# A hybrid encoder layer on one core: gate block maxima at heads five to eight, query and key rows of the second memory in other buffers, the first sequence's output begun behind its last row

## The chip, the core and the metric

The kernel runs on one core of a Trainium2 chip. The core has a matmul engine (TensorE, PE in the profile; PEld is its weight load), a vector engine (VectorE, DVE), an engine for activation functions and copies (ScalarE, ACT), a general-purpose engine (GpSimd, POOL) and an engine that here issues nearly all transfers (SyncE, SP). Each engine works through its own instructions in order and waits on semaphores for the others. The metric is the device time of one launch in microseconds (us); the three runs of the kernel before took 2096.93, 2098.42 and 2098.59 us, a median of 2098.42.

## What is computed

Two sequences of 512 tokens with 1024 channels go through the same encoder layer. In short:

```python
x = x + 0.5 * swiglu(rms_norm(x, ffn1_norm), ffn1_w_gate, ffn1_w_up, ffn1_w_down)
h = rms_norm(x, mix_norm)
aq, ak, av, mq, mk, mv, gate_pre, o_pre, g_att, g_mlstm = split(h @ w_in)
att = gqa_block_attention(rope(rms_norm(aq)), rope(rms_norm(ak)), av)      # 8 heads of 64, 2 key heads
mem = mlstm_bidirectional(mq, mk, mv, gate_pre, gate_bias, o_pre, head_norm)  # 4 heads of 128
merged = sigmoid(g_att) * (att @ w_up_att) + sigmoid(g_mlstm) * (mem @ w_up_mlstm)
x = x + merged @ w_out
x = x + 0.5 * swiglu(rms_norm(x, ffn2_norm), ffn2_w_gate, ffn2_w_up, ffn2_w_down)
y = rms_norm(x, final_norm)
```

Everything is float32. The memory (mlstm) has gates per token; for every memory head and each of its two directions the kernel needs the largest gate exponent in each block of 128 tokens, with and without a triangular mask. These are the block maxima of the title.

## The kernel before

**Precision.** A float32 operand is split into a high part and the rest (`split`, lines 656 to 658, and `split_w`, 236 to 241: ACT copies the high part, DVE subtracts), and a product is three matmuls: high by high, high by low, low by high. Weights of the mixing block are split once for the first sequence and parked in memory; the second sequence loads the two parts back (`load_w`, lines 247 to 263; in the profile `wpark<-w` at L262 and `w<-wpark` at L254).

**Stages.** The program starts with the first feed-forward block (FFN) of both sequences together, whose gate, up and down products go through a scheme that needs seven products where eight would do it directly. Then comes the mixing block (`mix`), as a generator for each sequence: `m0` for the first, `m1` for the second, which are advanced in turn, so that the second's projections run beside the first's output projection. Then comes the second FFN of both sequences together, and with its last products the final norm and the write-out.

**Order.** The instructions of one engine are not in the order of the text. A planner sorts them ahead of the launch: every instruction has a priority, which counts up along the text; `shifted(n)` adds n to it for a while (a positive number is later). An instruction that is ready may be taken ahead of one with an earlier priority that isn't. On the chip the planned order of each engine is fixed.

**Buffers.** On-chip memory is given out in rings by tag. Those that matter here: `wr`, four buffers for raw weights; `w8`, four buffers of twice that size for split weights; `t2` and `f2`, rows of 128 x 512; the banks `mm` (3), `s` (2, in the profile `pss`), `t` (2, `pst`) and `o` (1, `pso`) of the matmul's accumulators. `box` is one tile of eight rows, cut by hand into four rows for gate exponents (`eb`) and four for output gates.

**The mixing block**, as far as the change touches it. `gates` (line 860) computes the gate exponents and writes them to memory (`ebuf`). `mem_rows` (lines 956 to 964) loads one head's and direction's exponents into a row of `box` for all partitions (`box<-ebuf`, L959) and adds the mask (L963: on POOL for the first sequence, on DVE for the second). `mem_max` (lines 966 to 969) takes the block maxima of both rows with two DVE reductions into `n1` and `bd` (L968, L969; the tile is `st`). `mem_scales` (from line 971) makes the memory's scales out of all of them, and `mem_head` (from line 1102) uses these for a head: it loads the rows again, computes ACT exponentials (L1126), multiplies them with the product of the head's query and key rows (L1112, L1128), and `mem_out` turns the result and multiplies it with the values.

The query and key rows of memory head h come from two projections, `mem_qk(h, 0)` and `mem_qk(h, 1)` (line 909): each result is scaled (L914) and split into a high and a low row (L657, L658). The four rows lie in one tile of ring `w8`, `qks[h]`. For heads one and two they are projected before the attention, for heads three and four while the memory heads run.

The attention runs head by head: `scores(h + 1)` (matmuls L997 into the two `s` banks, row maximum on DVE L1000, exponential on ACT L1002, reciprocal and scaling on DVE L1003 and L1004), then `attend(h)` (turning L1016, split, product with the values L1024), then one `mem_max`, and then `fill`, which lets one or two further projections of the queue follow, one for the first four heads and two for the others.

**The start.** The first sequence's rows are turned on PE (`turn`, L1233), its norm factors are computed on DVE and ACT (`rows_rstd`), and `bcast_psum` (lines 209 to 214) brings the factors into all partitions with four transposes (L213); only then can DVE scale the rows (L1257).

**The end.** `ffn_down` (from line 505) runs 28 steps of four blocks of nine (or six) matmuls; every block ends in an addition on DVE (L606). The last rows of the first sequence come out of the last step but two (T4), the upper half of the second sequence's out of the last but one (T1), the rest out of the last (B22), which is cut in two halves of 256 columns. With each row of the first sequence `done2` adds its squares to a sum (`sq_add`, L155 on ACT and L156 on POOL). `finish0` computes the norm factor of the first sequence (`stats`: transposes L203, a reduction L205 and twelve small operations) and turns, scales (L1416) and writes its eight output tiles.

Of the kernel before, what the change touches and what calls it, by code (L numbers as in the profile page):

```python
# [9 lines left out]
F32R = mybir.dt.float32r  # L10
# [6 lines left out]
P = 128  # L17
S = 512
D = 1024
KD = D // P  # L20
# [6 lines left out]
def encoder(ctx, tc, I, outs):  # L27
    nc = tc.nc
# [3 lines left out]
    wpool = ctx.enter_context(tc.tile_pool(name="wpool", bufs=3))  # L32
# [9 lines left out]
    def nm(s):  # L42
        n_id[0] += 1
        return f"{s}_{n_id[0]}"

    @contextmanager
    def shifted(n):

        tc.cur_priority += n
        yield  # L50
        tc.cur_priority -= n
# [603 lines left out]
    def split(src, hi, lo, eng=None):  # L655

        nc.scalar.activation(hi, src, AF.Copy)  # L657
        (eng or V_).tensor_tensor(lo, src, f(hi), op=ALU.subtract)  # L658
# [101 lines left out]
    def mix(s, xh, xl, early=None, extra=None, after=None):  # L760
# [147 lines left out]

        def mem_qk(h, j):
            def done(pp):  # L910
                if j == 0:
                    qks[h] = wpool.tile([P, 4, S], F32R, tag="w8", bufs=4, name=nm("qk"))
                t = F2()
                V_.tensor_tensor(t, pp, R[s], op=ALU.mult)  # L914
                split(t, qks[h][:, 2 * j, :], qks[h][:, 2 * j + 1, :])
            return win_cols((768, 1280)[j] + h * P, done)

        ogs = {}
# [47 lines left out]
        def mem_max(h, d):  # L966
            eb3, em3 = mem_rows(h, d)
            V_.tensor_reduce(n1[:, d, :, h], em3, axis=AX.X, op=ALU.max)  # L968
            V_.tensor_reduce(bd[:, d, :, h], eb3, axis=AX.X, op=ALU.max)  # L969
# [78 lines left out]
        for h in range(HA):  # L1048
            nxt = scores(h + 1) if h + 1 < HA else None
            attend(h, Ps)  # L1050
            Ps = nxt
            with shifted(150):
                mem_max(h // 2, h % 2)
            fill(1 if h < 4 else 2)
            if h == 2 and extra:
                extra()
# [45 lines left out]
        def mem_head(h):  # L1102
            qk = qks[h]
            ebs, ems = zip(*[mem_rows(h, d) for d in range(2)])
            dn_ = small(8, "dn")
            dn = dn_.rearrange("p (d b) -> p d b", d=2)
            Ts = []
            for i in range(4):
                p = PS()
                isl = slice(i * P, (i + 1) * P)  # L1110
                for n, (a, b) in enumerate(((0, 2), (0, 3), (1, 2))):
                    nc.tensor.matmul(p, qk[:, a, isl], qk[:, b, :], start=(n == 0), stop=(n == 2))  # L1112
                pair = []
                for d in range(2):
                    W = T2()
                    st_ = i if d == 0 else 3 - i
                    for j in range(st_ + 1):
                        b = j if d == 0 else 3 - j
                        if j == st_:
                            src, bias = ems[d][:, j], bd[:, d, st_, h:h + 1]  # L1120
                        else:
                            src = ebs[d][:, j]
                            dist = st_ - j
                            bias = (n1[:, d, st_, h:h + 1] if dist == 1 else
                                    n2[:, d, st_, h:h + 1] if dist == 2 else n2[:, d, 1, h:h + 1])
                        nc.scalar.activation(W[:, b * P:(b + 1) * P], src, AF.Exp, bias=bias)  # L1126
                    cl = slice(0, (i + 1) * P) if d == 0 else slice(i * P, S)
                    V_.scalar_tensor_tensor(W[:, cl], p[:, cl], DM ** -0.5, W[:, cl], op0=ALU.mult, op1=ALU.mult,  # L1128
                                            accum_out=dn[:, d, st_:st_ + 1])
                    pair.append(W)  # L1130
                Ts.append(pair)
            V_.scalar_tensor_tensor(dn_, dn_, -1.0, dn_, op0=ALU.mult, op1=ALU.max)
            V_.tensor_tensor(dn, dn, en[:, :, :, h], op=ALU.max)
            V_.reciprocal(dn_, dn_)
            for i in range(4):
                tf, tb = Ts[i]
                rf, rb = dn[:, 0, i:i + 1], dn[:, 1, 3 - i:4 - i]
                lo_, di_, up_ = slice(0, (i + 1) * P), slice(i * P, (i + 1) * P), slice((i + 1) * P, S)
                nc.scalar.activation(tf[:, lo_], tf[:, lo_], AF.Copy, scale=rf)
                V_.scalar_tensor_tensor(tf[:, di_], tb[:, di_], rb, tf[:, di_], op0=ALU.mult, op1=ALU.add)  # L1140
                if i < 3:
                    V_.tensor_scalar(tf[:, up_], tb[:, up_], rb, None, op0=ALU.mult)
            return Ts
# [122 lines left out]
    for k, bank in enumerate((MM, PS, PT, MM, PS, PT, MM, PO)):  # L1266
        keep_x(0, k, turn(0, k, bank), x0r[k])
    W = [gu_left_a(raw0[0])]
    R0 = bcast_psum(rs)
    xc[B11], xc[B21] = xc_tile(), xc_tile()  # L1270

    def first_x(k):
# [188 lines left out]

    def done2(s, d, th):
        if s == 0:
            acc0[0] = sq_add(xs[0][:, d, :], acc0[0], "R")
        elif d == KD - 1:
            finish0()
            finish1_upper()
        elif th is not None:
            finish1(th)
# [44 lines left out]
```

## Time and profile before

| | |
|---|---|
| median of three runs | 2098.42 us |
| the profiled execution | 2097.18 us |
| its span, first to last instruction | 2095.4 us |
| its mean granted TensorE clock | 0.997 |
| PE busy | 2066.0 us (99%) |
| DVE busy | 1575.3 us (75%) |
| ACT busy | 895.9 us (43%) |
| POOL busy | 104.7 us (5%) |
| DMA moved | 458.53 MB, mean 219 GB/s |
| chain that ended last: PE | 90% |

A line of a timeline reads: start in us, duration in us, engine, line of the kernel, operation, what it writes <- what it reads, shapes, number of instructions put together; in brackets, the idle time of the engine before it and what ended that. On DVE and ACT the listed durations of instructions that follow each other overlap by some 0.1 us; from start to start a 128 x 512 operation on DVE takes 0.6 us. "SPq" is a transfer being issued by SP. A line of the waits reads: who <- for whom: us in total, times, longest. A line of a stretch of time reads: its bounds, its length, then busy time and number of instructions of PE, PEld, DVE, ACT and POOL, the granted clock of PE, the share of the DMA engines that was busy, and GB/s.

### The profile page before, as it was taken

The numbers are of one execution on the slowest core, as the hardware profiler recorded it, in microseconds if no ns is written. First come the engines' busy times: TensorE is split into PE (matmuls) and PEld (weight loads), VectorE is DVE, ScalarE is ACT, GpSimd is POOL, SyncE is SP. The second block draws the span as 40 slices with busy tenths as digits, with TensorE's granted clock in tenths as the row PEclk, the third lists the DMA queues.
The fourth block names the chain that finished last, engine by engine and source line by source line (L and its number), as shares of the span: only waits on it lengthen the run. The fifth ranks groups of instructions, "written<-read, shape, count | busy, mean of one in ns | idle before, by whom it ended". The sixth has DMA issues, their size and how long they took to land.

```text
span 2095.4 us, 27335 instructions
## 1 busy us (share of the span) xinstructions
PE 2066.0 (99%) x9488; PEld 1694.0 (81%) x9488; DVE 1575.3 (75%) x2866; ACT 895.9 (43%) x1645; POOL 104.7 (5%) x110
## 2 busy tenths in 40 slices
PE   8999999999999999999999999999999999999997
PEld 6888888888888777878887787888888888888886
DVE  7888988786797898575568745545888888786796
ACT  7544444442235566463334543323544444443222
POOL 0000000001003011000110000001000000000000
PEclk9999999999999999999999999999999999999999
DMA  9655655699767655769585354677656555599752
GB/s 282 200 179 183 204 170 181 208 348 352 259 229 253 212 180 176 260 229 302 176 298 165 101 172 157 204 247 248 207 171 212 190 173 181 190 348 348 259 192 110
DMA packets 304187, 458.53 MB, mean 219 GB/s; under 512 B 20305, under 2 KB 170849, under 8 KB 303025
## 3 DMA queue, kind: packets, MB, share of 16 engines
q1 hardware_dynamic: 303456, 455.52, 64.5%
q0 software_dynamic: 592, 1.27, 0.3%
q8 instruction: 75, 1.23, 0.3%
q14 instruction: 64, 0.52, 0.1%
HBM read 289.82 MB, written 166.89 MB: 218 GB/s over the span
## 4 chain that ended last, share of the span: by engine, by line
PE 90%; DVE 4%; DMA 3%; ACT 1%; issue 1%; SPq 0%; DVEq 0%; POOL 0%; ACTq 0%
PE mm L755 17%; PE pss L333 17%; PE pst L333 11%; PE mm L333 10%; PE mm L589 8%; PE pst L589 4%; PE pss L589 4%; PE mm L739 4%; PE pso L589 3%; PE pso L739 1%; PE pso L1024 1%; PE pst L1016 1%; PE pss L997 1%; PE pst L755 1%; PE pss L755 1%; PE pss L1112 1%
## 5 line engine op out<-in xcount | busy, mean ns | idle before, releaser
L755 PE MATMUL mm<-xh,w 128*128 128x512 f32 x896 | 293.2, 396 | 1.4 <-DMA w<-wpark 1.4
L333 PE MATMUL pss<-xc,w 128*128 128x512 f32 x1056 | 256.4, 392 | 0.3 <-DVE t L364 0.3
L333 PE MATMUL mm<-xc,w 128*128 128x512 f32 x1056 | 252.7, 390 | 1.6 <-ACT w L291 0.9
L333 PE MATMUL pst<-xc,w 128*128 128x512 f32 x1056 | 253.6, 389 | 0.0
L333 PEld LDWEIGHTS pss<-xc,w 128*128 128x128 f32 x1056 | 196.8, 188 | 47.7 <-DVE t L364 7.2
L333 PEld LDWEIGHTS mm<-xc,w 128*128 128x128 f32 x1056 | 197.4, 188 | 44.3 <-ACT w L291 1.8
L333 PEld LDWEIGHTS pst<-xc,w 128*128 128x128 f32 x1056 | 198.2, 188 | 41.2
L755 PEld LDWEIGHTS mm<-xh,w 128*128 128x128 f32 x896 | 168.1, 189 | 36.3 <-DMA w<-wpark 2.7
L589 PE MATMUL mm<-rt,w 128*128 128x512 f32 (+1 forms) x819 | 187.7, 383 | 0.0
L755 PE MATMUL mm<-xl,w 128*128 128x512 f32 x448 | 176.5, 394 | 0.0
L589 PEld LDWEIGHTS mm<-rt,w 128*128 128x128 f32 x819 | 150.6, 188 | 29.8
L291 ACT ACTIVATE w<-t 128x512 fp32r<-128x512 f32 x176 | 107.1, 627 | 140.5 <-issue 55.2
L292 DVE TENSOR_TENSOR w<-t,w 128x512 fp32r<-128x512 f32 x176 | 118.4, 688 | 50.3 <-ACT w L291 48.1
L333 PE MATMUL pss<-xc,f 128*128 128x512 f32 x528 | 126.8, 389 | 0.0
L333 PEld LDWEIGHTS pss<-xc,f 128*128 128x128 f32 x528 | 99.1, 188 | 20.6
L657 ACT ACTIVATE w<-wr 128x512 fp32r<-128x512 f32 x72 | 45.1, 632 | 138.3 <-PE pso L589 65.2
L755 PEld LDWEIGHTS mm<-xl,w 128*128 128x128 f32 x448 | 84.5, 189 | 16.7
L657 ACT ACTIVATE w<-t 128x512 fp32r<-128x512 f32 x82 | 51.8, 631 | 107.4 <-PE pst L589 62.4
L589 PE MATMUL pss<-rt,w 128*128 128x512 f32 x396 | 93.6, 389 | 0.0
L589 PE MATMUL pst<-rt,w 128*128 128x512 f32 x396 | 93.6, 389 | 0.0
L239 ACT ACTIVATE w<-wr 128x1024 fp32r<-128x1024 f32 (+1 forms) x56 | 57.3, 1028 | 74.5 <-PE mm L755 32.0
L589 PEld LDWEIGHTS pst<-rt,w 128*128 128x128 f32 x396 | 74.3, 188 | 15.4
(333 smaller groups left out, 3675.4 us busy)
## 6 DMA issues: line engine op xcount, KB each, us to landing
rt<-rbuf SPq DMA_DIRECT2D x154, 512.0 KB, 5.5
wpark<-w SPq DMA_DIRECT2D x104, 512.0 KB, 3.5
w<-wpark SPq DMA_DIRECT2D x104, 512.0 KB, 4.9
wr<-in_ffn_w_gate_dram SPq DMA_DIRECT2D x62, 512.0 KB, 5.5
rbuf<-tab SPq DMA_DIRECT2D x102, 256.0 KB, 4.3
wr<-in_ffn_w_up_dram SPq DMA_DIRECT2D x44, 512.0 KB, 4.6
rbuf<-f SPq DMA_DIRECT2D x72, 256.0 KB, 4.1
wr<-in_w_in_dram SPq DMA_DIRECT2D x36, 512.0 KB, 6.9
```

Of the source, the lines that this page charges most:

```text
L239: pin(nc.scalar.activation(hi, raw, AF.Copy))
L291: pin(nc.scalar.activation(t[:, 0], src, AF.Copy))
L292: pin(V_.tensor_tensor(t[:, 1], src, f(t[:, 0]), op=ALU.subtract))
L333: nc.tensor.matmul(p, a[:, k, :], xt[:, b, k, :], start=(first and k == 0 and i == 0), stop=(k == HK_ - 1 and i == 2), skip_group_check=True)
L589: nc.tensor.matmul(p, u[:, a, d * P:(d + 1) * P], r[:, b, ts], start=(first and q == 0 and k == 0), stop=(q == len(us) - 1 and k == 2), sk ...
L657: nc.scalar.activation(hi, src, AF.Copy)
L739: nc.tensor.matmul(p[b][:, :N], a[:, k, bs], w_[:, kl, :], start=(k == 0 and i == 0), stop=(k == KD - 1 and i == 2))
L755: nc.tensor.matmul(p, a[:, k, :], b, start=(k == 0 and i == 0), stop=(k == n - 1 and i == 2))
L997: nc.tensor.matmul(p, qT[:, h, b * P:(b + 1) * P], kv[:, hk * 2 + j, :], start=(j == 0), stop=(j == 1))
L1016: nc.tensor.transpose(p[:, b * P:(b + 1) * P], Ps[b][:, kb * P:(kb + 1) * P], ident)
L1024: nc.tensor.matmul(po, Vst[:, kv_, hk, :], w, start=(kv_ == 0 and i == 0), stop=(kv_ == 3 and i == 1))
L1112: nc.tensor.matmul(p, qk[:, a, isl], qk[:, b, :], start=(n == 0), stop=(n == 2))
```

## The change

Four things are changed.

1. `mem_max` is no longer called once after every attention head with a priority 150 later; it is called twice after each of heads five to eight, for both directions of memory head h - 4, with no shift.
2. In the second sequence (`s` is 1) the four rows of a memory head no longer lie in one tile of ring `w8`, but in two tiles of two rows, one for each projection, in ring `wr`. In the first sequence they stay where they were; the rows are only named one by one.
3. The broadcast of the first sequence's norm factors at the start of the program gets a priority 60 earlier.
4. `finish0` is called behind the first sequence's last row, in step T4, with a priority 100 later, and no longer behind the upper half of the second sequence's, in step T1. The sums of squares of its last four rows are added by DVE and no longer by POOL.

```diff
         def mem_qk(h, j):
             def done(pp):
-                if j == 0:
-                    qks[h] = wpool.tile([P, 4, S], F32R, tag="w8", bufs=4, name=nm("qk"))
+                if j == 0 and not s:
+                    t = wpool.tile([P, 4, S], F32R, tag="w8", bufs=4, name=nm("qk"))
+                    qks[h] = [t[:, i] for i in range(4)]
+                elif s:
+                    t = wpool.tile([P, 2, S], F32R, tag="wr", bufs=4, name=nm("qk"))
+                    qks.setdefault(h, []).extend(t[:, i] for i in range(2))
                 t = F2()
                 V_.tensor_tensor(t, pp, R[s], op=ALU.mult)
-                split(t, qks[h][:, 2 * j, :], qks[h][:, 2 * j + 1, :])
+                split(t, *qks[h][2 * j:2 * j + 2])
...
             attend(h, Ps)
             Ps = nxt
-            with shifted(150):
-                mem_max(h // 2, h % 2)
+            if h >= 4:
+                mem_max(h - 4, 0)
+                mem_max(h - 4, 1)
             fill(1 if h < 4 else 2)
...
                 for n, (a, b) in enumerate(((0, 2), (0, 3), (1, 2))):
-                    nc.tensor.matmul(p, qk[:, a, isl], qk[:, b, :], start=(n == 0), stop=(n == 2))
+                    nc.tensor.matmul(p, qk[a][:, isl], qk[b], start=(n == 0), stop=(n == 2))
...
-    R0 = bcast_psum(rs)
+    with shifted(-60):
+        R0 = bcast_psum(rs)
...
         if s == 0:
-            acc0[0] = sq_add(xs[0][:, d, :], acc0[0], "R")
+            acc0[0] = sq_add(xs[0][:, d, :], acc0[0], "R", eng=V_ if d >= DH else None)
+            if d == KD - 1:
+                with shifted(LATER):
+                    finish0()
         elif d == KD - 1:
-            finish0()
             finish1_upper()
```

## The prediction

> **What bounds the kernel now.** I read the page first, then the waits of the matmul engine over the whole span, and then the stretches of time in which those waits lie.
>
> ```profile
> span 2095.4 us, 27335 instructions
> PE 2066.0 (99%) x9488; PEld 1694.0 (81%) x9488; DVE 1575.3 (75%) x2866; ACT 895.9 (43%) x1645; POOL 104.7 (5%) x110
> ```
>
> PE (TensorE) is busy 99% of the span, and the change takes no matmul away. So it can only win what PE loses: 2095.4 - 2066.0 = 29.4 us of idle time, about 10 us of it the last write-out after the last matmul, and whatever PE does at a lowered clock. The waits (total, times, longest, in us) say where:
>
> ```profile
> PE pss L997 <- ACT t L1002: 3.4, 2, 3.1
> PE pst L937 <- DVE t L658: 1.9, 2, 1.2
> PE pss L1405 <- DVE xs L606: 1.4, 1, 1.4
> PE mm L755 <- DMA w<-wpark: 1.4, 3, 0.7
> ```
>
> L997 is the score matmul of an attention head, L937 the turning of the queries, L1405 the last write-out, L755 a projection that waits for parked weights. Four stretches of time (length, busy time of PE, PEld, DVE, ACT, POOL, then granted clock, DMA share, GB/s) show what stands behind them: heads one to four of the first and of the second sequence, heads five to eight of the second, and the stretch before the end.
>
> ```profile
> 706.00:760.00 54.00, 52.81 (x258) 41.56 (x257) 53.03 (x101) 31.98 (x68) 6.86 (x5) 1.00 0.61 195
> 1106.00:1160.00 54.00, 50.09 (x230) 39.46 (x230) 48.57 (x123) 26.98 (x62) 0.00 (x0) 0.94 0.51 155
> 1160.00:1216.00 56.00, 55.81 (x282) 43.96 (x281) 34.89 (x69) 27.50 (x59) 0.70 (x1) 1.00 0.35 117
> 2066.60:2086.20 19.60, 17.19 (x141) 16.02 (x139) 17.32 (x54) 5.85 (x21) 0.00 (x0) 1.00 0.33 122
> ```
>
> In heads one to four DVE is full (53.03 of 54, 48.57 of 54) and PE loses 1.2 and 3.9 us; in heads five to eight of the second sequence DVE has 21 us to spare and PE loses 0.2. Before the end DVE is again close to full and PE loses 2.4.
>
> **Part 1, the block maxima, second sequence.** This is the largest term. PE, at the first head's scores:
>
> ```profile
> 1106.05 1.07 PE L997 MATMUL pss<-kv,qT 128*128 128x512 f32 x4
> ...
> 1108.54 0.39 PE L755 MATMUL mm<-xl,w 128*128 128x512 f32 x1
> 1112.05 0.89 PE L997 MATMUL pss<-kv,qT 128*128 128x512 f32 x2 [3.12 <-ACT t L1002]
> ...
> 1115.42 0.45 PE L1016 MATMUL pst<-ident,t 128*128 128x128 f32 x1 [0.77 <-DVE asm L1003]
> ```
>
> ```profile
> 1112.00:1120.00 8.00, 7.18 (x21) 5.24 (x21) 4.76 (x13) 2.23 (x6) 0.00 (x0) 0.57 0.81 267
> ```
>
> Two gaps, 3.12 and 0.77 us, and then a granted clock of 0.57: 7.18 us of matmul time at 0.57 loses 7.18 x 0.43 = 3.1 us more. What DVE did meanwhile, and what SP issued:
>
> ```profile
> 1108.05 0.69 DVE L963 TENSOR_TENSOR box<-box,tab 128x512 f32<-128x512 f32 x1 [0.37 <-DMA box<-ebuf]
> 1108.66 0.68 DVE L969 TENSOR_REDUCE st<-box 128x4 f32<-128x512 f32 x1
> 1109.26 0.68 DVE L968 TENSOR_REDUCE st<-box 128x4 f32<-128x512 f32 x1
> 1109.85 0.68 DVE L914 TENSOR_TENSOR f<-mm,R 128x512 f32<-128x512 f32 x1
> 1110.45 0.68 DVE L1000 TENSOR_REDUCE asm<-pss 128x1 f32<-128x512 f32 x1
> ```
>
> ```profile
> 1104.27 3.74 SPq L232 DMA_DIRECT2D wr<-in_ffn_w_gate_dram  x1
> 1108.12 1.79 SPq L959 DMA_DIRECT2D box<-ebuf  x1
> ```
>
> L963, L968 and L969 are one block maximum (mem_max). L1000, the row maximum of the first scores, has its first bank from about 1106.6 on (two of the four matmuls at 1106.05) and runs at 1110.45 behind two of these maxima, one of which waits for its DMA; the DMA of the next sits behind a weight transfer that holds SP for 3.74 us. The scores that find no bank start at 1112.05, which is 1.6 us after L1000. Without the maxima L1000 follows L914 at about 1107.5, and the scores start near 1109.1, right behind the last L755: of the 3.12 us some 0.2 stay. So the gain is 2.9 + 0.77 + 3.1: **-6.8 us**. The bounds are -7.0, all of it, and 0 when the maxima stay where they are (first rival). Moved to heads five to eight they are the same 8 x 3 instructions of 0.6 us each, 14.4 us, against the 21 us that DVE has idle there, and PE has two filling projections a head to cover them.
>
> The Trainium skill, "TensorE: Matmul & The Clock Gate", sections "HAM oscillation — how this bites in real kernels" and "What's actually happening", says that an idle gap of some 3.4 us puts the matmul clock back to half, and that about 3.4 us of work restore it. The 0.57 behind a gap of 3.12 us agrees in kind. By its figure the lowered clock would cost 3.4 x 0.5 = 1.7 us (an estimate from that page) instead of 3.1, and the whole sum would come out 1.4 us smaller; this case's row lasts longer, and I go by the row.
>
> **Part 1, first sequence.** Here the adds (L963) run on POOL and only the two reductions on DVE.
>
> ```profile
> 704.55 0.63 PE L937 MATMUL pst<-ident,t 128*128 128x128 f32 x4 [1.16 <-DVE t L658]
> ```
>
> ```profile
> 701.70 0.68 DVE L969 TENSOR_REDUCE st<-box 128x4 f32<-128x512 f32 x1
> ...
> 714.36 0.67 DVE L968 TENSOR_REDUCE st<-box 128x4 f32<-128x512 f32 x1
> ```
>
> One reduction of 0.6 us stands on DVE in front of each of the two splits (L658) that PE waits for (1.9 us together). Taking both away: **-1.2 us**; bounds -1.9 and 0. The sixteen reductions do not get fewer; in heads five to eight they compete with the same attention work, for which the third rival has the price. The scales that follow the maxima (mem_scales) come later, and so do the first memory head's exponentials; 96 matmuls of the value projection lie beside them and cover that.
>
> **Part 2, the other buffers.** In the second sequence the split query and key rows of a memory head leave ring w8 (four buffers, which the projections' weights share; two are held by these rows) for ring wr. Four buffers instead of two then prefetch parked weights. What waits for them now:
>
> ```profile
> 1295.62 0.50 PE L755 MATMUL mm<-xh,w 128*128 128x512 f32 x1 [0.67 <-DMA w<-wpark]
> ...
> 1296.84 0.73 PE L755 MATMUL mm<-xh,w 128*128 128x512 f32 x2 [0.48 <-DMA w<-wpark]
> ```
>
> ```profile
> SPq L254 <- PE mm L755: 102.8, 21, 11.8
> ```
>
> SP's weight loads spend 102.8 us waiting for a buffer that a projection still reads, so depth is what they lack. I take the two gaps at 1295, **-1.1 us**; bounds -1.4 (all three waits) and, when ring wr now holds up another weight, +4.7 (second rival). The instruction count and every size stay the same. Ring wr also carries the second FFN's first four raw weights, which were fetched around 1104 (row above) and now come after these rows; PE does not reach that FFN before 1430, so 100 us cover them, and the burst of 4 x 512 KB leaves the place where it delayed box<-ebuf.
>
> **Part 3, the first broadcast.** Its four transposes get a priority 60 earlier, past the eight turns of the input (48 instructions and the two of the split).
>
> ```profile
> 12.82 0.16 DVE L192 SCALAR_TENSOR_TENSOR rs<-rs,rs 128x4 f32<-128x4 f32 x1
> ```
>
> ```profile
> 14.63 0.60 PE L213 MATMUL pst<-ident,rs 128*128 128x128 f32 x4
> ```
>
> ```profile
> 22.69 11.60 PE L333 MATMUL mm<-xc,w 128*128 128x512 f32 x49 [0.89 <-ACT w L291]
> ```
>
> ```profile
> 19.94 1.06 ACT L291 ACTIVATE w<-wr 128x1024 fp32r<-128x1024 f32 x1 [0.45 <-DMA wr<-in_ffn_w_gate_dram]
> ```
>
> The factor is ready at 12.98 and is turned at 14.63, so DVE's scaling can start up to 1.65 us earlier. But the second weight lands at 19.9 whatever is done, and the gap that ends at 22.69 hangs on its split, so little of that reaches PE: **-0.5 us**; bounds -1.5 (the 0.89 and a gap of the same kind before it) and +0.4 (one turn of 0.43 us delayed for nothing).
>
> **Part 4, the first sequence's output.** finish0 is issued behind the last row of that sequence, a step (four blocks of nine matmuls) earlier, with priority +100, and its last four sums go from POOL (1.29 us each) to DVE (0.6), idle there.
>
> ```profile
> 2060.22 1.29 POOL L156 TENSOR_TENSOR R<-R,f 128x512 f32<-128x512 f32 x1 [0.49 <-ACT f L155]
> ```
>
> ```profile
> 2066.63 0.60 PE L203 MATMUL pst<-ident,R 128*128 128x128 f32 x4
> ```
>
> ```profile
> 2078.26 1.08 DVE L606 SCALAR_TENSOR_TENSOR xs<-mm,xs 128x256 f32<-128x256 f32 x3
> ```
>
> The sums are complete at 2061.5, but their transposes (L203) come only after the step, at 2066.6; 8 outputs, 12 small operations and 4 products then keep DVE occupied until 2078.26, and PE waits 1.44 us for L606. finish0 counts 65 instructions itself and a block of the step 10, so +100 puts its transposes before the last block, 9 x 0.227 = 2.0 us earlier, not five. That can remove the 1.44 and a 0.41 beside it, less the 0.43 us of transposes that push that last block: **-1.3 us**. Bounds: -2.4 (all that PE loses in that stretch) and +2, should three outputs of 0.66 us slip behind the last step. The last chain, from the last matmul to the last write, does not change.
>
> **Sum.** -6.8 - 1.2 - 1.1 - 0.5 - 1.3 = -10.9 us. The profiled execution took 2097.2 us around its span, 1.2 us under the median of 2098.42; set against that median the forecast is 2098.4 - 10.9 = **2087.5 us**.
>
> **First rival: the maxima stay where they were.** The order is planned by readiness as well as by priority, and an idle DVE takes what is ready.
>
> ```profile
> 1085.95 0.68 DVE L968 TENSOR_REDUCE st<-box 128x4 f32<-128x512 f32 x1
> ```
>
> This maximum ran 20 us before the first score, though it is written behind a head and 150 later. Then the stall at 1108 stays, in its place or a little beside it, and so do the reductions in the first sequence; 1.1 + 0.5 + 1.3 = 2.9 us are left: 2095.5. Against it speaks that at equal readiness L1000 now goes first and that the weight burst has gone from there.
>
> **Second rival: ring wr holds up the output projection.** The planner hands out a ring's buffers in program order.
>
> ```profile
> 984.23 0.46 SPq L232 DMA_DIRECT2D wr<-in_w_out_dram  x1
> ```
>
> ```profile
> 1044.11 0.63 ACT L657 ACTIVATE qk<-f 128x512 fp32r<-128x512 f32 x1 [3.58 <-DVE f L914]
> 1044.64 1.04 ACT L239 ACTIVATE w<-wr 128x1024 fp32r<-128x1024 f32 x1
> ```
>
> ```profile
> wr<-in_w_out_dram SPq DMA_DIRECT2D x8, 512.0 KB, 4.6
> ```
>
> Four of its weights were fetched by 984. Now the first head's query rows come between the first and the second of them, and they are split only at 1044.1. If the second is fetched after that, 4.6 us of transfer and 1.04 + 1.2 of splitting end at 1050.9, and the second unit is due once the first has run its 24 matmuls of 0.227 us from 1042.7 on, at 1048.2: 2.7 us of gap, with 3.1 for the clock at worst 5.8. The weight gain of 1.1 turns into a loss of 4.7: 2098.4 - 10.9 + 5.8 = 2093.3. Against it, the loads before it let SP pass at 1029, so on the chip the fetch can run ahead of its planned place, and gates and key turns can fill the gap.
>
> **Third rival, slower: the stall moves along.** In heads five to eight two maxima follow each other in every head, each add (L963) behind a DMA that is planned shorter than it is (1.79 us held on SP above), and in order on DVE ahead of the next head's L1000. Each time that DVE is held for 3 us or more while both score banks are full costs what it cost here, 6.8 us. One such head leaves 2094.3, two give 2101.1, three 2107.9; from two on it is slower. For it speaks that the price needs only one late transfer; against it the 21 us of idle DVE, the fact that seven of the eight adds before cost PE little, and that all four slots of these rows are free for the first pair.
>
> **Chances.** Forecast 0.42, with its own range 2083 to 2092; first rival 0.24; second 0.12; third 0.17 (two heads 0.09); 0.05 for nothing or something else. About 0.2%, 4.2 us, is what can be told from no change: faster means under 2094.2, slower over 2102.6. Faster: 0.42 + 0.12 + 0.05 of the first rival = 0.59. Slower: 0.17, and 0.03 of the rest, 0.20. Same: 0.21. The range reaches from the forecast with the larger bounds, 2083.5, to the third rival with two heads, 2102: some 0.8.
>
> **What would show it.** Right: no PE wait for L1002 above 0.5 us and a clock of 1.00 in heads one to four of the second sequence; no L968 or L969 in front of the query splits of the first; no PE wait on w<-wpark; L203 of the end near 2 us before the last block of its step is over and no PE wait for L606. Wrong: L963 on DVE before the second sequence's first L1000, a wait of L997 in heads five to eight, or a gap in front of the second output projection.

## The result and the profile after

The changed kernel took 2086.73 us (median of four runs, 2084.75 to 2090.09) against 2098.51 us (median of four, 2096.93 to 2099.41) of the kernel before on the same chip: 11.8 us less, a ratio of 0.9946 (95% interval 0.9929 to 0.9964). The forecast was 2087.5. The profiled execution of the changed kernel took 2090.09 us and is the slowest of its four, so its trace shows 7.2 us of the 11.8. The top of its page and four of PE's waits:

```profile
span 2088.2 us, 27312 instructions
PE 2063.1 (99%) x9488; PEld 1694.4 (81%) x9488; DVE 1573.0 (75%) x2870; ACT 894.6 (43%) x1645; POOL 100.3 (5%) x106
```

```profile
PE mm L755 <- DMA w<-wpark: 2.0, 2, 1.5
PE pst L1020 <- DVE t L658: 1.1, 2, 0.8
...
PE pso L1028 <- DVE t L658: 0.6, 1, 0.6
...
PE pss L1411 <- ACT f L1437: 0.4, 1, 0.4
```

The lines have moved by four or five: the score matmul is L1001, the row maximum L1004, the maxima are L967 (add), L972 and L973, their loads L963. The 3.4 us of the score matmul's wait are gone, and so are the 1.4 for L606; of the 1.9 of the query turns (L941) 0.3 are left. The wait for parked weights is still there, longer, and in another place. The stretches of time that the prediction showed, of the changed kernel (the last one moved with the end):

```profile
706.00:760.00 54.00, 53.05 (x268) 42.39 (x267) 51.11 (x104) 34.31 (x73) 2.59 (x2) 1.00 0.55 172
1106.00:1160.00 54.00, 54.00 (x263) 43.74 (x262) 48.43 (x112) 26.82 (x62) 0.00 (x0) 1.00 0.43 147
1160.00:1216.00 56.00, 55.31 (x280) 44.01 (x279) 43.94 (x100) 30.48 (x68) 0.69 (x1) 1.00 0.42 132
2059.31:2078.91 19.60, 18.91 (x151) 17.56 (x149) 16.93 (x54) 5.58 (x21) 0.00 (x0) 1.00 0.29 108
```

PE loses nothing in 1106 to 1160, where it lost 3.9 us and 3.1 more to the clock; it loses 0.7 in heads five to eight, where it lost 0.2, and 0.7 instead of 2.4 before the end. So PE's picture is the forecast one. DVE's is not: of the second sequence's sixteen reductions nine run between 1121.6 and 1156.2, among heads one to four, and DVE is as busy there as before (48.43 and 48.57 us). They lie behind the first row maxima, but not behind heads five to eight, where their calls stand. What brought this about is another question, and the timelines of DVE and SP in front of the second sequence's first scores give the first hint:

```profile
1110.17 0.69 DVE L918 TENSOR_TENSOR f<-mm,R 128x512 f32<-128x512 f32 x1 [3.30 <-PE mm L755]
1110.78 1.28 DVE L1004 TENSOR_REDUCE asm<-pss 128x1 f32<-128x512 f32 x2
...
1121.59 0.67 DVE L972 TENSOR_REDUCE st<-box 128x4 f32<-128x512 f32 x1
```

```profile
1096.22 14.74 SPq L254 DMA_DIRECT2D w<-wpark  x9
1111.05 0.86 SPq L963 DMA_DIRECT2D box<-ebuf  x2
```

DVE sits idle for 3.30 us before L918, with no maximum in sight, and takes the first two row maxima at 1110.78, 0.81 us after the scores began (1109.97). SP issues nine weight transfers in a row and only then the loads of the maxima's rows. Before, weight transfers, row loads and the second FFN's burst alternated there. The order of SP has changed, and it is not plain from this trace which of the parts did that.

For the comparison of all runs I cut each profiled execution at the same matmuls: the last of the first FFN, the first and last of the first sequence's output projection, the first of the second sequence's, the first of the second FFN and of its down part, the last of all. The lengths between them (us, by PE's timelines; without the two output projections, 52.2 to 53.1 and 43.5):

| kernel | start and first FFN | first mixing | second mixing | second FFN, up | its down part and end |
|---|---|---|---|---|---|
| before | 656.2 | 386.5 | 303.9 | 422.6 | 220.98 |
| changed | 658.0 | 384.9 | 297.8 | 423.7 | 218.85 |

### The profile page after: what moved, and what is told of

Read it like the earlier page. It is cut to its first block, busy times and chain, and to the rows that moved or that the text cites. A ratio compares the mean times of both kernels' runs of the same rounds, so it can differ in the third digit from the quotient of the medians.

```text
span 2088.2 us, 27312 instructions
## 1 busy us (share of the span) xinstructions
PE 2063.1 (99%) x9488; PEld 1694.4 (81%) x9488; DVE 1573.0 (75%) x2870; ACT 894.6 (43%) x1645; POOL 100.3 (5%) x106
## 4 chain that ended last, share of the span: by engine, by line
PE 90%; DVE 4%; DMA 3%; ACT 1%; issue 1%; SPq 0%; DVEq 0%; POOL 0%; ACTq 0%; POOLq 0%
PE mm L755 18%; PE pss L333 17%; PE pst L333 11%; PE mm L333 9%; PE mm L589 9%; PE pst L589 4%; PE pss L589 4%; PE mm L739 4%; PE pso L589 3%; PE pso L739 1%; PE pso L1028 1%; PE pso L1167 1%; PE pss L1001 1%; PE pst L755 1%; PE pss L755 1%; PE pss L1117 1%
## 5 line engine op out<-in xcount | busy, mean ns | idle before, releaser
L240 DVE TENSOR_TENSOR w<-wr,w 128x1024 fp32r<-128x1024 f32 (+1 forms) x56 | 69.6, 1243 | 23.6 <-ACT w L239 22.9
```

The source lines that it names most:

```text
L240: pin(lo_eng.tensor_tensor(lo, raw, f(hi), op=ALU.subtract))
```

## Experiments: one part taken back

Four kernels are the changed one with one part undone; their own runs of the kernel before had a median of 2097.68 (15 runs).

**Without part 1** (the maxima called as before):

```diff
-            if h >= 4:
-                mem_max(h - 4, 0)
-                mem_max(h - 4, 1)
+            with shifted(150):
+                mem_max(h // 2, h % 2)
```

> The changed kernel without the moved maxima: one after every head, 150 later, as before. My theory: the stall in front of the second sequence's first scores comes from the maxima that stand on DVE ahead of the first row maximum; it returns, with the two reductions in the first sequence, 6.8 + 1.2 us, so some 2094.7 against 2098.5 before, and the profile shows L1001 waiting for about 3 us with a clock near 0.6 behind it. Rival: it was the burst of four weights of the second FFN that made the maxima's transfers late, and the other ring for the query and key rows has moved that burst away: then the stall stays away and the time is near 2088.

Measured: 2086.34 us (2085.22 to 2088.04), ratio 0.9949 [0.9936, 0.9961]: as fast as with the part. First mixing 388.2, second 294.4. Two of PE's waits, and DVE at the second sequence's first row maxima:

```profile
PE pst L941 <- DVE t L658: 2.9, 3, 1.8
PE pst L1020 <- DVE t L658: 2.4, 4, 0.8
```

```profile
1109.51 0.69 DVE L918 TENSOR_TENSOR f<-mm,R 128x512 f32<-128x512 f32 x1 [3.30 <-PE mm L755]
1110.12 1.28 DVE L1004 TENSOR_REDUCE asm<-pss 128x1 f32<-128x512 f32 x2
...
1114.23 0.68 DVE L967 TENSOR_TENSOR box<-box,tab 128x512 f32<-128x512 f32 x1
```

In the first sequence the waits for the query splits are back (L941); in the second no stall returns. The first maximum there (L967) runs at 1114.23, behind the first row maxima, although its call stands where it stood before. So the largest term of the prediction does not belong to the call's place.

**Without part 2** (the second memory's rows in w8 again):

```diff
-                if j == 0 and not s:
-                    t = wpool.tile([P, 4, S], F32R, tag="w8", bufs=4, name=nm("qk"))
-                    qks[h] = [t[:, i] for i in range(4)]
-                elif s:
-                    t = wpool.tile([P, 2, S], F32R, tag="wr", bufs=4, name=nm("qk"))
-                    qks.setdefault(h, []).extend(t[:, i] for i in range(2))
+                if j == 0:
+                    qks[h] = wpool.tile([P, 4, S], F32R, tag="w8", bufs=4, name=nm("qk"))
...
-                split(t, *qks[h][2 * j:2 * j + 2])
+                split(t, qks[h][:, 2 * j, :], qks[h][:, 2 * j + 1, :])
```

> The changed kernel with the query and key rows of the second memory in ring w8 as before. My theory: the maxima alone clear the stall in front of the first scores. In the changed kernel the ring wr costs a gap of 2.0 us in front of the first key projection of the second sequence and 1.7 us of lowered clock behind it; here that goes, and the two waits for parked weights of 1.1 us come back: about 2084 (2.6 us faster than the changed kernel). Rival: with two buffers held the weights come late in more places, and the time is 2088 or more.

Measured: 2093.12 us (2090.73 to 2095.62), ratio 0.9980 [0.9971, 0.9989]; first mixing 385.3, second 303.6. PE's waits, and DVE's timeline up to the first row maximum:

```profile
PE pss L997 <- ACT t L1002: 3.5, 1, 3.5
...
PE pst L1016 <- DVE asm L1003: 1.2, 1, 1.2
```

```profile
1105.21 0.69 DVE L963 TENSOR_TENSOR box<-box,tab 128x512 f32<-128x512 f32 x1 [0.88 <-DMA box<-ebuf]
...
1108.35 0.69 DVE L963 TENSOR_TENSOR box<-box,tab 128x512 f32<-128x512 f32 x1 [0.66 <-DMA box<-ebuf]
1108.96 0.68 DVE L969 TENSOR_REDUCE st<-box 128x4 f32<-128x512 f32 x1
1109.55 0.68 DVE L968 TENSOR_REDUCE st<-box 128x4 f32<-128x512 f32 x1
1110.14 0.68 DVE L914 TENSOR_TENSOR f<-mm,R 128x512 f32<-128x512 f32 x1
1110.74 1.28 DVE L1000 TENSOR_REDUCE asm<-pss 128x1 f32<-128x512 f32 x2
```

The calls stand behind heads five to eight here, and the maxima run in front of the first head all the same. The whole stall is there, as in the kernel before: the scores began at 1105.96, and DVE comes to them 4.8 us later, behind two maxima whose adds wait for their loads (0.88 and 0.66 us). The forecast of 2084 missed; its rival, 2088 or more, came.

**Without part 3** (the broadcast where it was) and **without part 4** (finish0 where it was, the four sums on POOL):

```diff
-    with shifted(-60):
-        R0 = bcast_psum(rs)
+    R0 = bcast_psum(rs)
```

> The changed kernel with the first broadcast at its old priority. Forecast: a loss of 0.5 us against the changed kernel, 2087.2. Rival, from the profile of the changed kernel, where the first FFN stands 1.5 us later than before: the earlier broadcast costs 1.5 to 1.7 us, and without it the time is 2085.1. Third: the start varies from run to run by as much, and nothing can be told.

```diff
-            acc0[0] = sq_add(xs[0][:, d, :], acc0[0], "R", eng=V_ if d >= DH else None)
-            if d == KD - 1:
-                with shifted(LATER):
-                    finish0()
+            acc0[0] = sq_add(xs[0][:, d, :], acc0[0], "R")
         elif d == KD - 1:
+            finish0()
```

> The changed kernel with the first sequence's output begun where it was before, and its sums on POOL. Forecast by the profile of the changed kernel, whose last step ends 1.9 us earlier against the start of the last products: a loss of 1.3 to 2.0 us, 2088.0 to 2088.7, and PE again waits 1.4 us for L606 near the end. Rival: the gain at the end is given back in the last write-out, and the time stays at 2086.7.

Measured: 2084.74 (2082.41 to 2086.3), ratio 0.9939 [0.9927, 0.9952] without part 3, and 2088.52 (2087.39 to 2089.6), ratio 0.9957 [0.9945, 0.9970] without part 4. In the latter this wait of PE is back, and the last stage is 220.99 us long, as before:

```profile
PE pss L1411 <- DVE xs L606: 1.4, 1, 1.4
```

The last stage is the steadiest of all: in the fourteen profiled executions of this study it took 218.85 to 218.88 with part 4 and 220.97 to 220.99 without it. Part 4 is worth 2.1 us.

## Experiments: one part alone

> The kernel before with part 2 alone (query and key rows of the second memory in ring wr). Theory of the prediction, the maxima's place in the text is what counts: only the two gaps at 1295 go, 1.1 us, so about 2096.5 against 2097.7, and the stall of 3 us or more stays at the first scores of the second sequence. Theory after the first runs, the buffers carry the gain: the block maxima of the second sequence go behind its first scores by themselves, no wait of L1001 for L1006 above 0.5 us, and 2086 to 2089 (the changed kernel without the move of the maxima, 2086.3, plus 1.8 for the tail, less 0 to 2 for the broadcast).

Part 2 alone: 2090.02 us (2086.85 to 2090.37) against 2098.06, ratio 0.9959 [0.9946, 0.9972]: 8.0 us. The second mixing block is 295.0 long, and no wait of the score matmul is left.

> The kernel before with part 1 alone, the maxima called after heads five to eight. In the planned order the second sequence's maxima still stand ahead of its first row maximum. Theory now (the call's place moves only the first sequence's maxima; in the second one the buffers decide): the first mixing block gets 2.2 us shorter, the stall of 3 to 3.5 us at the second sequence's first scores stays, about 2095.9 against 2098.1. Theory of the prediction (the call's place removes the stall too): 2098.1 - 6.8 - 1.2 = 2090.

Part 1 alone: 2096.2 us (2094.32 to 2097.79) against 2098.54, ratio 0.9989 [0.9981, 0.9998]: 2.3 us. The stall is still there, in one piece:

```profile
1113.65 0.99 PE L997 MATMUL pss<-kv,qT 128*128 128x512 f32 x2 [3.72 <-ACT t L1002]
```

By the means over all profiled executions, what part 1 gains lies in the first sequence. There the first mixing block took 384.7 to 386.5 us in the nine profiled kernels that have it, 385.5 in the mean, and 386.5 to 388.2, mean 387.7, in the five that don't: 2.2 us, where single executions of one kind differ by 1.7.

> The kernel before with part 3 alone, the earlier broadcast. The prediction: 0.5 us faster (bounds -1.5 and +0.4). What the other runs suggest: the last matmul of the first FFN ends at 656.6 to 658.3 in the six that have the earlier broadcast and at 656.2 to 657.7 in the six that don't (means 657.3 and 656.8), and the changed kernel without it was 2.0 us faster; so 0.5 to 2 us slower, 2098.5 to 2100.5 against 2098.3. Third possibility: the first weight rows land at different times from one execution to the next and the part has no effect that can be told from that, 2097.5 to 2099.

Part 3 alone: 2098.41 (2095.72 to 2103.28) against 2098.11, ratio 1.0003 [0.9994, 1.0012]. (The kernels without the broadcast in that expectation were seven, not six; their mean is the 656.8 it gives.) The three possibilities can't be told apart within that interval, but a gain of 0.2% is excluded. PE at the start:

```profile
13.58 1.06 PE L213 MATMUL pst<-ident,rs 128*128 128x128 f32 x4
...
17.40 0.49 PE L333 MATMUL mm<-xc,w 128*128 128x512 f32 x1 [0.25 <-ACT xc L278]
```

The transposes come 1.05 us earlier than before (14.63), but the first product of the FFN begins at 17.40 instead of 17.29. DVE's first scaling (L1257) starts at 14.74 instead of 15.34; ACT's split (L278), for which the product waits, starts at 16.72 instead of 16.56, right behind ACT's copies (L1238) of the turns that had to step back.

Alone, parts 1, 2 and 3 give -2.3, -8.0 and +0.3, and part 4, by taking it back, -1.8; that adds up to -11.8, what the whole change gives. Each of these differences is uncertain by some 2 to 4 us, so the exactness is luck. Taken back one at a time, the parts come by the ratios to -0.6, -7.1, +1.5 and -2.3, some -8.5 in all. Whether the parts need each other is therefore open.

## Experiments: what part 2 does

Part 2 changes three things in that place at once: the weight burst of the second FFN (four 512 KB transfers) goes from 1104 to 1305 and later, w8 has four buffers for weights instead of two, and the maxima come later. The burst and the maxima were each moved without the other two; the deeper buffers were tried only with the burst gone.

**The burst alone.** In the kernel before, the four fetches wait for a value that `mem_scales` writes:

```diff
+            late[:] = [en[:, 0, 0, 0:1]]
...
-    raw0 = up.fetch(0)
+    raw0 = up.fetch(0, behind=late[0])
...
-    W += [up.left(j) for j in (1, 2)]
+    W += [up.left(j, late[0]) for j in (1, 2)]
```

> The kernel before, with its buffers and maxima, but the four first weights of the second FFN are fetched behind the second sequence's scales (mem_scales) and no longer at 1103 to 1112. Theory A, the stall comes from maxima that stand on DVE ahead of the first row maximum, whatever their loads do: the stall of 3 us and the lowered clock stay, 2096 to 2098. Theory B, it comes from the weight burst that makes the loads box<-ebuf late: the maxima stay where they are (first ones from 1085 on) but end earlier, the wait of L998 for L1003 falls under 1 us, 2090 to 2093. Theory C, it comes from the two buffers of w8 that the weights of the second sequence have: no difference, 2097 to 2098.

Measured: 2095.26 us (2092.75 to 2099.09), ratio 0.9986 [0.9978, 0.9995]. Timelines of SP, DVE and PE:

```profile
1103.59 7.88 SPq L959 DMA_DIRECT2D box<-ebuf  x4
```

```profile
1107.44 0.69 DVE L963 TENSOR_TENSOR box<-box,tab 128x512 f32<-128x512 f32 x1 [1.50 <-DMA box<-ebuf]
...
1112.22 1.28 DVE L1001 TENSOR_REDUCE asm<-pss 128x1 f32<-128x512 f32 x2
```

```profile
1113.83 1.22 PE L998 MATMUL pss<-kv,qT 128*128 128x512 f32 x2 [2.99 <-ACT t L1003]
```

The burst has gone from there (to 1161), the stall stays. SP issues the four row loads over 7.88 us, each in 0.32 us with waits between them, and DVE still comes to the first row maximum 4.3 us after the scores began (1107.96). Theory B falls as the cause of the stall. The 2.8 us by which the median is lower were not traced to a place, since the profiled execution is the slowest of eleven.

**The maxima alone.** The changed kernel with the buffers of before, but every load of a maximum's row in the second sequence waits, by a copy of one column, for attention rows:

```diff
-        def mem_rows(h, d):
+        def mem_rows(h, d, behind=None):
...
+            if behind is not None:
+                V_.tensor_copy(eb[:, 0:1], behind)
...
-            eb3, em3 = mem_rows(h, d)
+            eb3, em3 = mem_rows(h, d, f(att[:, (h + 3) // 2, 0, 0:1]) if s else None)
```

> The changed kernel with the buffers of before (like the run without part 2, 2093.1), but each load of a maximum's row in the second sequence now also waits for the attention rows of a head before (a copy of one column on DVE), so that the maxima can't run before heads four to seven have done. The weight burst stays ahead of the first scores. Theories A and B both: no maximum on DVE ahead of the first scores, no wait of the score matmul above 0.5 us, 2086 to 2089. Theory C, depth of w8: the stall of 3.5 us at 1112 stays, about 2093. Third rival of the prediction: a stall moves into heads five to eight, 2093 or more.

Measured: 2094.79 us (2093.1 to 2097.61), ratio 0.9986 [0.9978, 0.9995]. The stall at 1112 is gone, though ring w8 is as shallow as before and the burst stands in front of the scores (at 1079 to 1097): theory C falls too. But heads five to eight have stalls of their own. DVE and PE:

```profile
1189.07 0.69 DVE L965 TENSOR_TENSOR box<-box,tab 128x512 f32<-128x512 f32 x1 [1.31 <-DMA box<-ebuf]
...
1192.02 0.69 DVE L965 TENSOR_TENSOR box<-box,tab 128x512 f32<-128x512 f32 x1 [1.06 <-DMA box<-ebuf]
...
1193.88 0.67 DVE L1002 TENSOR_REDUCE asm<-pss 128x1 f32<-128x512 f32 x1
```

```profile
1195.48 0.73 PE L999 MATMUL pss<-kv,qT 128*128 128x512 f32 x2 [2.26 <-ACT t L1004]
...
1228.97 0.96 PE L1115 MATMUL pss<-qk 128*128 128x512 f32 x3 [1.75 <-DVE t L1131]
```

That is the third rival of the prediction, made to happen: two adds wait for their loads in front of a row maximum, and the scores stand. In the changed kernel itself it did not come (0.7 us lost in heads five to eight, above).

**Deeper buffers, early maxima.** The changed kernel, but the first two rows of memory head one lie in w8, so that ring wr is free for the output projection's weights:

```diff
-                    t = wpool.tile([P, 2, S], F32R, tag="wr", bufs=4, name=nm("qk"))
+                    t = wpool.tile([P, 2, S], F32R, tag="wr" if h or j else "w8", bufs=4, name=nm("qk"))
```

> The changed kernel, but the first two query rows of memory head one of the second sequence lie in ring w8 and no longer in wr, so that all four of wr are free for the output projection's weights. The planned order then has no gap for them: PE's waits for w<-wpark in front of the second sequence's first key projection (2.0 us) and the lowered clock behind them (1.7) should go, 2083 to 2084 against 2086.7. In this order the maxima's loads stand early again (ahead of the second sequence's key weights), but the weight burst is still gone: theory A, maxima on DVE ahead of the first row maximum, expects the stall back, 3 to 6.8 us on top, 2086 to 2090; theory B, the burst, expects no wait of the score matmul above 1 us.

Measured: 2089.38 us (2085.39 to 2093.01), ratio 0.9961 [0.9949, 0.9972]. PE and the stretch behind:

```profile
1113.24 1.22 PE L1001 MATMUL pss<-kv,qT 128*128 128x512 f32 x2 [4.34 <-ACT t L1006]
```

```profile
1112.00:1120.00 8.00, 6.76 (x20) 5.36 (x21) 5.89 (x15) 3.38 (x9) 0.00 (x0) 0.58 0.57 156
```

The stall is back, 4.34 us and a clock of 0.58 behind it, with no burst and with more buffers than before: theory A as expected. The gaps for w<-wpark at 1096 are gone, as expected too. So one tile decides both: with memory head one's first rows in wr, the maxima are planned behind the first scores and the key weights come late; with them in w8, the other way round.

**Both held.** The same pin, but on the rows of heads one and two, with the buffers of before, and then with the rows as in the last kernel (both without part 3):

```diff
-            eb3, em3 = mem_rows(h, d)
+            eb3, em3 = mem_rows(h, d, f(att[:, 0, 0, 0:1]) if s else None)
```

> The buffers of before, no earlier broadcast, the tail of the changed kernel, and the second sequence's maxima held by data: each load of their rows waits for the attention rows of heads one and two (a copy of one column), so that they run from head three on and not as late as in the run that held them to heads five to eight. The weight burst stays where it was. If DVE's order in front of the first row maximum is the whole cause, the wait at 1112 and the lowered clock are gone and nothing comes in their place: 2093.1 - 6.8 = 2086.3, and 2085 to 2088 in all. If the deeper w8 is needed too, the second mixing block stays over 300 us long (303.9 before, 294 to 298 with part 2) and the time over 2090.

> The changed kernel without the earlier broadcast, with the first two query rows of memory head one of the second sequence in w8 (so that ring wr is free for the output projection's weights), and the second sequence's maxima held by data behind heads one and two. Stall at the first scores (4.3 us in the run with those rows in w8 and the maxima early) gone, and the gap in front of the first key projection (2.0 us and the clock) gone too: 2083 to 2085, no slower than the changed kernel without the broadcast (2084.7). If the maxima between the heads' row maxima cost PE as they did in heads five to eight (2.3 us and the clock behind it), 2087 to 2089.

Measured: 2091.48 us (2088.4 to 2094.23), ratio 0.9967 [0.9955, 0.9979], and 2087.68 us (2086.83 to 2088.14), ratio 0.9947 [0.9935, 0.9960]. The first missed its 2085 to 2088; it lies over 2090, but the second mixing block is 299.0 us long and not over 300. The second missed its 2083 to 2085 and lies in the 2087 to 2089 of its other case. The stretch of the old stall in the first of them, and what PE waits for later:

```profile
1112.00:1120.00 8.00, 8.00 (x40) 6.33 (x40) 7.35 (x17) 5.07 (x13) 0.00 (x0) 1.00 0.39 130
```

```profile
1163.64 0.50 PE L1026 MATMUL pso<-t,kv 128*128 128x512 f32 x1 [1.00 <-ACT t L657]
...
1258.50 0.73 PE L755 MATMUL mm<-xh,w 128*128 128x512 f32 x2 [0.75 <-DMA w<-wpark]
...
1289.30 0.50 PE L755 MATMUL mm<-xh,w 128*128 128x512 f32 x1 [0.64 <-DMA w<-wpark]
```

Where no maximum stands in front of the row maxima, PE is busy for the whole stretch at full clock; the price comes later, in heads five to eight (from 1160 to 1200 PE was busy 38.40 of 40 us here, 37.57 in the second kernel), and in the memory heads, where the shallow w8 leaves its gaps. The four kernels make a square for the second mixing block:

| | maxima in front of the first scores | maxima behind them |
|---|---|---|
| buffers of before | 303.6 | 299.0 |
| rows in wr but for the first two | 300.3 | 296.0 |
| all rows in wr, no pin (the changed kernel, those without part 1, 3 or 4, and part 2 alone) | - | 294.3 to 297.8 |

By these single profiled executions, holding the maxima back gives 4.6 and 4.4 us, with the pin's price in it, and the buffers give 3.3 and 3.0. By the ratios to the kernel before it is 2.8 us for the pin (0.9980 to 0.9967, and 0.9961 to 0.9947; the intervals overlap) and 4.1 for the buffers (0.9980 to 0.9961, and 0.9967 to 0.9947). The two in the right column also lack part 3, for which nothing was measured.

PE's idle time in that block is 6.3 and 4.6 us in the upper row and 4.4 and 2.5 in the lower one. The lowered clock takes another 2.8 us in each kernel of the left column, and nothing in the right one. That is 4.6 and 4.7 us for the maxima's place, and 2.0 and 2.1 from row to row; the further 1 us from row to row is busy time of PE and was not traced. The rows differ in the burst's place too (1079 to 1112 in the upper one, behind 1300 in the lower one), so what is put down to the buffers includes it.

## Why the prediction was right, and where it was wrong

The time was right; the working was right about the stall and wrong about what moves it. In that term the time came out by luck: the stall went by part 2, which stood in the sum at -1.1.

**The stall's mechanism holds.** The row maximum "runs at 1110.45 behind two of these maxima": in each of the six kernels that have maxima there (before, without part 2, parts 1 and 3 alone, the late burst, the first rows in w8) PE waited 2.26 to 4.34 us at the second sequence's first scores, and the clock of the eight microseconds from 1112 on was between 0.57 and 0.79. In the eight others there is no such wait.

**The step that failed** is "Part 1, the block maxima, second sequence", -6.8 us: that a call behind heads five to eight moves them. The first rival's objection, that the planner takes what is ready, is what happens in the second sequence. I put against it that "at equal readiness L1000 now goes first"; but in the kernel without part 2 the first add of the second sequence runs at 1084.9, 21 us before the first scores, so no score was ready beside it for priority to decide. By itself the call's place gives the second sequence nothing (second mixing 303.9 before, 303.6 without part 2), or little (301.9 with part 1 alone, with the stall still in it).

**Part 2** stood in the sum at -1.1, with bounds of -1.4 and +4.7, and brings 8.0 us. Two things are in that. The depth of w8, for which I priced the two gaps at 1295, is one. The same stretch in both traces, before and after:

```profile
1200.00:1328.00 128.00, 125.80 (x593) 101.30 (x592) 71.61 (x205) 53.98 (x136) 3.37 (x4) 1.00 0.53 173
```

```profile
1200.00:1328.00 128.00, 127.92 (x611) 104.30 (x610) 74.63 (x212) 56.97 (x140) 3.25 (x4) 1.00 0.59 185
```

PE's idle time falls from 2.2 to 0.1 us: the three gaps for parked weights (0.28, 0.67, 0.48) and one of 0.76 for L1128 that I had not counted. The last does not come back in the kernel without part 2, whose w8 is as shallow as before, so it is not shown to come from the depth. The other part was not in my list of edges at all: which buffers a projection's rows take decides when SP is planned to be free, and with it when rows of quite another tile are loaded. I saw that the burst would leave its place, and gave it no price.

**The second rival came true in another place.** The first sequence's output projection, for which I had 2.7 us of gap, ran without one (52.2 us, before 52.6). But ring wr did hold something up, the key weights of the second sequence:

```profile
1096.64 0.47 PE L755 MATMUL mm<-xh,w 128*128 128x512 f32 x1 [1.55 <-DMA w<-wpark]
...
1097.80 1.18 PE L755 MATMUL mm<-xh,w 128*128 128x512 f32 x2 [0.46 <-DMA w<-wpark]
```

```profile
1098.00:1100.00 2.00, 2.00 (x5) 1.58 (x6) 0.00 (x0) 0.00 (x0) 0.00 (x0) 0.50 1.01 339
1100.00:1102.00 2.00, 2.00 (x7) 1.55 (x6) 0.00 (x0) 0.00 (x0) 0.00 (x0) 0.68 0.99 363
```

2.0 us of gap and 2 x 0.50 + 2 x 0.32 = 1.6 of clock, 3.6 us in this execution; in the four others with all rows in wr the gaps before 1105 were 0.5 to 1.6 us in all and the clock stayed at 1.00. With the first two rows in w8 they are gone.

**Smaller terms.** First sequence: -1.2 forecast, -2.2 by the means, more than the 1.9 of the two waits that I took as the bound; where the rest comes from was not tried. Broadcast: -0.5 forecast, nothing measurable; "up to 1.65 us earlier" was right for the transposes (1.05), but the turns that they pass, copied on ACT, stand on the way of the first product, which I had as the upper bound (+0.4). End: -1.3 forecast, -2.1 measured; I took off 0.43 us for transposes that push a block back, but these run in both kernels, so they need cost nothing new. Which of part 4's two edits gives the gain was not tried. L203 came where it was put:

```profile
2059.42 0.27 PE L203 MATMUL pst<-ident,R 128*128 128x128 f32 x1
```

That is 199.2 us after the down part's first product, 201.3 before: the 2.0 us that the working gave.

**Two sums.** The larger bounds add up to -14.2 us, which is 2084.2 and not 2083.5. The chance of "slower" counts the third rival whole, though by its own price one head of it, 2094.3, would have been "same".

**Open.** How the planner's own reckoning gets from one tile in wr to the later row loads wasn't tried, and no kernel had the deeper w8 with the burst in its old place. Of the twelve variants none is faster than the changed kernel beyond what can be measured; the lowest is the one without the broadcast, 2084.74 with an interval that overlaps.

## What to carry to other kernels

A sum can be right while its largest term stands under the wrong edit: undo the parts one at a time before believing the attribution. In a planned order, later in the text need not be later on the engine: with part 1 alone the first sequence's maxima began at 751.6 instead of 701.7, the second's at 1086.9 instead of 1085.9. What was ready early ran early there, and only a dependency (data, or a buffer that is not free) held it back. And when an edit changes which ring a tile lies in, list every transfer that shares the issuing queue with that ring's users, since their order moves too.

## What was unexpected of the hardware

The granted clock fell to 0.50 for 3.4 us (1097.87 to 1101.29) behind two gaps of 1.55 and 0.46 us, 0.7 us apart (1096.64 and 1097.80 above), and not at all in the same place in the kernel without part 1, whose gaps were 0.67 and 0.44 us. The Trainium skill, "TensorE: Matmul & The Clock Gate", section "HAM oscillation — how this bites in real kernels", warns of idle gaps of more than about 3.4 us; here 2.0 us in all, in two pieces, were enough.

The same price was not always paid. Behind the 3.72 us of part 1 alone the clock stood at 0.50 for 3.4 us (1113.93 to 1117.35), all of it work, and 1.7 us were lost; behind the single 2.99 us of the late burst it stood there for 6.8 us (1112.80 to 1119.63), of which 5.80 were work, and 2.9 us were lost. The times at which the clock changes lie whole multiples of 3.41 us apart in each trace. Cut into stretches of 3.41 us at these times, all fourteen traces agree between 20 and 2060 us: the clock fell behind each of the eight stretches in which PE was idle for 1.96 to 3.13 us in all, and behind none with 1.75 us or less. It came back behind the first stretch in which PE was busy throughout: after one stretch in three cases, and after two in the five whose first stretch still held 0.77 to 1.28 us of idle time. The section "What's actually happening" of the same page of the Trainium skill lets about 3.4 us of sustained work restore the clock, and these eight cases agree.
